# Gated-delta inverse: the diagonal blocks of 16 solved on VectorE by way of DRAM, and the attention mixer's product queued behind the matrix

## The chip, the cores and the metric

The kernel runs on one core of a Trainium2 chip. The metric is the device time of one execution in microseconds (us). The five engines of a core have queues of their own and run in order: PE (TensorE, matrix products and transposes), DVE (VectorE), ACT (ScalarE), POOL (GpSimd) and SP (SyncE, which here issues the DMAs). PSUM is the memory into which TensorE writes; it is used here as eight banks, in four pairs named acc, pc, pd and pa.

## The reference

A stack of four layers over 256 tokens of width 1024. Two layers, called "first" here, hold four mixers on a quarter of the width each (a: HGRN2, b: gated linear attention, c: latent attention, d: the gated delta rule), then an output product `w_out` and a feed-forward part. Two more layers of another kind follow, which the change does not touch. Mixer d computes, for each chunk of 64 tokens and each of 4 heads:

```
kb = kc * bt[..., None]
m = jnp.where(strict, jnp.einsum('nbhid,nbhjd->nbhij', kb, kc) * lmask, 0.0)
rhs = jnp.concatenate([vc * bt[..., None], kb * jnp.exp(b)[..., None]], axis=-1)
sol = lax.linalg.triangular_solve(m + eye, rhs, left_side=True, lower=True, unit_diagonal=True)
u, w = sol[..., :dv], sol[..., dv:]
a_qk = jnp.einsum('nbhid,nbhjd->nbhij', qc, kc) * lmask
...
v_new = u_ - jnp.einsum('bhcd,bhdv->bhcv', w_, state)
o = (jnp.einsum('bhcd,bhdv->bhcv', q_ * jnp.exp(b_)[..., None], state)
     + jnp.einsum('bhij,bhjv->bhiv', a_, v_new))
```

The kernel takes chunks of 128 tokens, so there are 2 chunks and 4 heads: 8 unit lower triangular matrices of 128x128 to be inverted in each first layer.

## The kernel before

**Weights.** All weights are fp32 and come from DRAM through SP's queue into `raw` (three buffers, 512 KB each at the most). ACT rounds each to `wh` (L302), VectorE or POOL makes the rest `wl` = raw - wh (L305), and a product is three passes on TensorE (`mm3`, L331 to L333): wh with the high part, wl with the high part, wh with the low part. A buffer of `raw` comes free when its `wl` is made, and the next weight's DMA waits for that.

**What sets the order.** A tile scheduler, driven by a simulated timeline, puts each engine's instructions in one fixed order. The mixers are generators that are advanced in phases (`PLAN1` = d, b, a, c; `RUN1`): d's preparation, b's projection, d's inverse, a's projection, b's end, c, c's attention, a's end. Each engine then does its list in order, so an instruction that waits holds back all behind it on that engine.

**Mixers a and b** are the work that surrounds d on VectorE: for each level of a tree over the chunk `gl_e` (L723, L729) and `gl_r` (L735) are made on VectorE, multiplied on TensorE (L745, L753) and written under a mask into `gl_a` (copies under a predicate, L762); then the values are applied (L770, L771), and the head's norm (L603 to L610: `hn_sq` on ACT, `hn_ssq`, `hn_y`, `hn_o` on VectorE) and the transposed result `mT` (L417 to L420) follow.

**Mixer d.** For each chunk t, L1129 multiplies K and Q with the transposed K, and L1130, L1131 multiply by the decay: `MT`, the negated strict part, transposed, and `AT` for the output. The transposed K (`kT`, L1104 and L1118) is laid out with zeros, so that a product over all 128 partitions takes one head's 64. The inverse goes by doubling of blocks: `V` begins as the identity with the blocks of 2 filled in (L1148, L1157), `T` holds the transposed diagonal blocks that a level needs (L1147, L1156, L1153). Six levels follow, w = 2, 4, ..., 64. A level below 32 multiplies MT by T (L1178), masks the result to `X` (L1179, on VectorE), multiplies V by X (L1193) and adds it into V (L1194, VectorE), then transposes V (L1199) into the next T (L1201, ACT). The levels 32 and 64 do the same on partial products and end on ACT (L1170, L1173, L1186, L1190). The output begins at L1207 and L1212 for chunk 0 and goes on with the state S0 (L1220), wT (L1229) and chunk 1.

**Mixer c** begins with a product of the input by 416 columns (`pz`), whose PSUM banks are one of `acc` and one of `pa`, in rotation.

Of the kernel before, what the change touches and what calls it, by code (L numbers as in the profile page):

```python
# [26 lines left out]
NEG = -1e30  # L27
# [34 lines left out]
def host_constants():  # L62
# [79 lines left out]
class K:  # L142
    def __init__(self, ctx, tc, a):
# [7 lines left out]
        self.ps = e(tc.tile_pool(name="ps", bufs=1, space=PSUM))  # L151
        self.units, self.made, self.nexti, self.emitted = [], {}, 0, 0
# [740 lines left out]
    def mixer_c(self, l, xT):  # L893
# [12 lines left out]
        pz = self.tm(xT, (("c", l), 2, 416))  # L906
# [93 lines left out]
    def mixer_d(self, l, xT):  # L1000
# [3 lines left out]
        code = [self.z([128, 16], "b_code", "b") for _ in range(2)]  # L1004
# [38 lines left out]
        def prep(t):  # L1043
# [5 lines left out]
            nbeta = self.s(4, "d_nbeta")  # L1049
            nc.vector.tensor_scalar(nbeta, beta, -1.0, None, op0=OP.mult)  # L1050
# [42 lines left out]
            nc.vector.tensor_tensor(kb, qk[:, 4:8], bc4(nbeta, 64), OP.mult)  # L1093
# [9 lines left out]
            kT = self.z([128, 2, 2, 128], "d_kT")  # L1103
            nc.gpsimd.memset(kT, 0.0)  # L1104
# [11 lines left out]
            for par in range(2):  # L1116
                rr = slice(par * 64, par * 64 + 64)
                nc.scalar.activation(kT[rr, par], p2[rr, :2], AF.Copy)  # L1118
            if t:
                o["qeT"] = self.z([128, 2, 128], "d_qeT")  # L1120
                nc.scalar.activation(o["qeT"], p2[:, 2:], AF.Copy)
# [22 lines left out]
        for t in range(2):  # L1144
            T[t] = self.z([128, 4, 64], "d_T")
            V[t] = self.z([128, 4, 128], "d_V")
            nc.gpsimd.tensor_copy(part(T[t], 2), half(mb(self.ident), 2, 0))  # L1147
            nc.gpsimd.tensor_copy(V[t], mb(self.ident))  # L1148
        for t in range(2):
            MT = st[t]["MT"]  # L1150
            p = four()
            for h in range(4):
                nc.tensor.transpose(p[:, h], MT[:, h], self.ident)  # L1153
            at = lambda i, n: self.cu[:, i * 64:i * 64 + 64].rearrange("p (b s) -> p b s", s=n)[:, None].to_broadcast(
                [128, 4, 64 // n, n])
            nc.vector.copy_predicated(part(T[t], 2), at(6, 2), half(p, 2, 0))  # L1156
            nc.vector.copy_predicated(half(V[t], 1, 1), at(5, 1), half(MT, 1, 1))  # L1157
        for lv in range(6):
            w = 2 << lv
            X = [None] * 2  # L1160
            for t in range(2):
# [17 lines left out]
                nc.vector.tensor_tensor(half(X[t], w, 0), part(p, w), half(mb(ms[:, lv * 128:lv * 128 + 128]), w, 0), OP.mult)  # L1179
            for t in range(2):  # L1180
                p = self.pt()[:, :256].rearrange("p (h i) -> p h i", h=4)
                if w >= 32:
# [11 lines left out]
                nc.vector.tensor_tensor(v, v, part(p, w), OP.add)  # L1194
# [37 lines left out]
        nc.scalar.activation(wT[:64], pw, AF.Copy)  # L1232
# [573 lines left out]
```

## Time and profile before

| | |
|---|---|
| median of 3 runs | 1531.69 us (1529.27 to 1532.72) |
| profiled execution, its own time | 1533.64 us |
| its span | 1531.9 us |
| busy: PE / DVE / ACT / POOL | 1477.8 / 1061.0 / 841.5 / 282.0 us |
| mean granted clock of TensorE | 0.992 |
| layer 0: first d_MT (L1130); first matmul of the output (L1207) | 86.5; 151.1 us |
| layer 0: the last masked copy of mixer a (L762) ends | 160.5 us |
| layer 1: first d_MT (L1130); L1207 | 472.4; 543.4 us |

The profiled execution took 1533.64 us, of which 1531.9 us lie between its first and its last instruction. The busy time of PE counts matmuls whose ends are modelled, so that a stretch with PE at 99% need not be at TensorE's peak. The two first layers are alike in their order; the stretches that the change touches lie at about 85 to 160 us and 470 to 553 us.

### The profile page before, as it was taken

To read this page: it belongs to the slowest core of one execution; us is meant where nothing else is said; L and a number is where in the kernel's file an instruction comes from. 1 tells how busy PE (TensorE), PEld (TensorE's weight loads), DVE (VectorE), ACT (ScalarE), POOL (GpSimd) and SP (SyncE) were. 2 spreads that over 40 slices of the span, in tenths; PEclk is the share of its full clock that TensorE was granted. 3 is DMA by queue.
4 is the path that set the end of the run, shared out by engine and by line. 5 is a ranking of instruction groups with operands and counts; after the bars stand their busy time and mean duration, and the time that the engine had idled before them with its cause. 6 is when DMAs were issued, how large, how long until landed. Compare 5 with 4: busy or idle time off the path is not lost.

```text
span 1531.9 us, 23533 instructions
## 1 busy us (share of the span) xinstructions
PE 1477.8 (96%) x8718; PEld 1278.7 (83%) x8727; DVE 1061.0 (69%) x1895; ACT 841.5 (55%) x1528; POOL 282.0 (18%) x379
## 2 busy tenths in 40 slices
PE   7999999999998999999999989999999999999998
PEld 7988888888897987888878878888877888788886
DVE  6897467767689666767676876566656695666655
ACT  5735356556565444655545674544554675544553
POOL 1553210000244332000042132000024231100010
PEclk9999999999999999999999999999999999999999
DMA  7523046666452213666646343666654543466663
GB/s 239 150 85 111 30 139 182 200 188 207 134 167 82 83 58 111 191 189 187 204 132 196 95 138 104 192 193 190 209 184 127 164 125 110 131 193 190 190 203 105
DMA packets 156417, 233.98 MB, mean 153 GB/s; under 512 B 11700, under 2 KB 118158, under 8 KB 156302
## 3 DMA queue, kind: packets, MB, share of 16 engines
q1 hardware_dynamic: 156302, 232.48, 49.2%
q8 instruction: 68, 1.11, 0.3%
q14 instruction: 47, 0.39, 0.1%
HBM read 231.40 MB, written 1.05 MB: 152 GB/s over the span
## 4 chain that ended last, share of the span: by engine, by line
PE 75%; DVE 12%; ACT 5%; POOL 2%; DMA 2%; issue 2%; SPq 0%; ACTq 0%; DVEq 0%; POOLq 0%
PE pa L377 8%; PE pd L377 8%; PE acc L333 6%; PE acc L331 6%; PE acc L332 6%; PE pc L331 5%; PE pc L333 5%; PE pc L332 5%; PE pa L378 4%; PE pd L378 4%; DVE wl L305 3%; PE pa L331 3%; PE pa L333 3%; PE pa L332 3%; DMA raw<-in_w_in_dram 2%
## 5 line engine op out<-in xcount | busy, mean ns | idle before, releaser
L305 DVE TENSOR_TENSOR wl<-raw,wh 128x1024 fp32r<-128x1024 f32 (+4 forms) x424 | 484.7, 1151 | 308.9 <-ACT wh L302 307.3
L302 ACT ACTIVATE wh<-raw 128x1024 fp32r<-128x1024 f32 (+4 forms) x420 | 432.9, 1035 | 368.0 <-PE pc L333 90.9
L305 POOL TENSOR_TENSOR wl<-raw,wh 128x1024 fp32r<-128x1024 f32 (+1 forms) x26 | 61.7, 2373 | 640.6 <-ACT wh L302 640.5
L377 PE MATMUL pa<-xT,wh 128*128 128x512 f32 x392 | 146.0, 398 | 0.0
L377 PE MATMUL pd<-xT,wh 128*128 128x512 f32 x392 | 145.7, 397 | 0.0
L378 PE MATMUL pa<-xT,wl 128*128 128x256 f32 x392 | 110.2, 281 | 0.2 <-DVE wl L305 0.2
L378 PE MATMUL pd<-xT,wl 128*128 128x256 f32 x392 | 110.2, 281 | 0.0
L377 PEld LDWEIGHTS pd<-xT,wh 128*128 128x128 f32 x392 | 73.7, 188 | 15.3
L377 PEld LDWEIGHTS pa<-xT,wh 128*128 128x128 f32 x392 | 73.7, 188 | 13.9
L332 PE MATMUL acc<-wl,f_h 128*128 128x512 f32 x200 | 78.0, 390 | 0.0
L332 PE MATMUL pc<-wl,f_h 128*128 128x512 f32 x200 | 77.8, 389 | 0.0
L333 PE MATMUL acc<-wh,f_l 128*128 128x512 f32 x200 | 77.3, 391 | 0.4 <-DVE f_l L1302 0.4
L333 PE MATMUL pc<-wh,f_l 128*128 128x512 f32 x200 | 77.5, 389 | 0.0
L378 PEld LDWEIGHTS pa<-xT,wl 128*128 128x128 f32 x392 | 74.1, 189 | 3.7 <-DVE wl L305 0.4
L378 PEld LDWEIGHTS pd<-xT,wl 128*128 128x128 f32 x392 | 74.1, 189 | 3.3
L331 PE MATMUL acc<-wh,xT 128*128 128x512 f32 (+4 forms) x200 | 70.8, 357 | 1.4 <-ACT xT L512 1.1
L332 PE MATMUL acc<-wl,xT 128*128 128x512 f32 (+4 forms) x200 | 70.6, 354 | 1.5 <-DVE wl L305 1.5
L331 PE MATMUL pc<-wh,f_h 128*128 128x512 f32 x200 | 71.4, 390 | 0.0
L333 PE MATMUL acc<-wh,xT 128*128 128x512 f32 (+4 forms) x200 | 70.2, 353 | 0.8 <-DVE xT L514 0.8
L331 PE MATMUL acc<-wh,f_h 128*128 128x512 f32 x200 | 67.0, 391 | 0.0
L331 PE MATMUL acc<-wh,mT 128*128 128x512 f32 (+2 forms) x136 | 51.1, 384 | 1.4 <-ACT mT L512 1.1
L332 PE MATMUL acc<-wl,mT 128*128 128x512 f32 (+2 forms) x136 | 51.1, 376 | 0.0
(660 smaller groups left out, 3843.4 us busy)
## 6 DMA issues: line engine op xcount, KB each, us to landing
raw<-in_w_in_dram SPq DMA_DIRECT2D x84, 512.0 KB, 3.7
raw<-in_w_mlp_up_dram SPq DMA_DIRECT2D x64, 512.0 KB, 3.8
raw<-in_w_mlp_down_dram SPq DMA_DIRECT2D x64, 512.0 KB, 3.6
raw<-in_ffn_w_gate_dram SPq DMA_DIRECT2D x44, 512.0 KB, 3.6
raw<-in_ffn_w_up_dram SPq DMA_DIRECT2D x44, 512.0 KB, 3.6
raw<-in_ffn_w_down_dram SPq DMA_DIRECT2D x44, 512.0 KB, 3.6
raw<-in_w_out_dram SPq DMA_DIRECT2D x32, 512.0 KB, 3.5
raw<-in_w_ple_gate_dram SPq DMA_DIRECT2D x16, 512.0 KB, 4.8
```

The source lines that it names most:

```text
L302: nc.scalar.activation(h[:, p], raw[:, p], AF.Copy)
L305: e.tensor_tensor(l[:, p], raw[:, p], h[:, p].bitcast(F), OP.subtract)
L331: t.matmul(out, ah, bh, start=first, stop=False, skip_group_check=True)
L332: t.matmul(out, ah, bl, start=False, stop=False, skip_group_check=True)
L333: t.matmul(out, al, bh, start=False, stop=last, skip_group_check=True)
L377: t.matmul(out[f], h[:, k, c], xT.both[:, :, kk], start=kk == 0, stop=False, skip_group_check=True)
L378: t.matmul(out[f][:, 1], l[:, k, c], xT[0][:, kk], start=False, stop=kk == 7, skip_group_check=True)
```

## The change

1. MT is no longer negated (`kb` takes beta; the signs go to VectorE's subtraction at the end of a level and to a scale of -1 in three copies on ACT).
2. `kT` is no longer laid out with zeros: one copy by ACT, and the products take slices of 64 partitions. POOL's memset of kT goes.
3. The diagonal blocks of 16 (64 of them in a layer: 8 matrices with 8 blocks) are inverted on VectorE. MT is written to a DRAM buffer `scr` (two DMAs of 256 KB), read back as `Z`, one block to a partition (1024 runs of 64 bytes), solved in `Y` by seven steps of two small instructions and four instructions of 64x512, and Y is written to a second DRAM buffer `scv` (1024 runs of 64 bytes). `V` is loaded from there (two DMAs of 256 KB). Levels w = 2, 4 and 8, and the copies that began them, go; w = 16, 32 and 64 stay as they were.
4. `scv` is set to zero once at the start, by four DMAs of 129 KB each. The tables lose 384 columns of bf16 in `cb` and 64 of fp32 in `cu`.
5. Mixer c's product takes both banks of `acc` and stands, on TensorE, behind the last product of L1129 (`lastmat`). The tile `code` gets buffers of its own.

```
+        zero = self.z([128, 258], "zero", "d")
+        nc.gpsimd.memset(zero, 0.0)
+        for i in range(4):
+            nc.sync.dma_start(self.at(self.scv, i * 128 * 258, [[258, 128], [1, 258]]), zero)
...
-        pz = self.tm(xT, (("c", l), 2, 416))
+        with self.tc.issue_after(self.lastmat.ins):
+            pz = self.tm(xT, (("c", l), 2, 416), outs=self.first_banks("acc"))
...
-                    nc.tensor.matmul(p[:, f], kT[:, par, f], qkT[:, f], start=True, stop=True)
+                    self.lastmat = nc.tensor.matmul(p[:, f], kT[rr, f], qkT[rr, f], start=True, stop=True)
...
+        dense = lambda m, t: self.at(m, t * 4 * 129 * 128, [[128, 128], [129 * 128, 4], [1, 128]])
+        blocks = lambda m: self.at(m, 0, [[16 * 129, 64], [128, 16], [1, 16]])
+        for t in range(2):
+            nc.sync.dma_start(dense(self.scr, t), st[t]["MT"])
+        Z, Y = self.z([64, 256], "d_Z"), self.z([64, 256], "d_Y")
+        nc.sync.dma_start(Z.rearrange("p (j r) -> p j r", r=16), blocks(self.scr))
+        nc.gpsimd.tensor_copy(Y, self.cb[:64, 512:768])
+        tmp, U = self.z([64, 512], "d_tmp"), self.z([64, 64], "d_U")
+        for r in range(1, 8):
+            p = tmp[:, :2 * r * r].rearrange("p (a c j) -> p a c j", a=2, c=r)
+            nc.vector.tensor_tensor(p, view(Z, r, [[136, 2], [0, r], [16, r]]), view(Y, 0, [[136, 2], [16, r], [1, r]]), OP.mult)
+            nc.vector.tensor_reduce(view(Y, r, [[136, 2], [16, r]]), p, AX.X, OP.add, negate=True)
+        p = tmp.rearrange("p (c r j) -> p c r j", c=8, r=8)
+        nc.vector.tensor_tensor(p, view(Y, 0, [[16, 8], [0, 8], [1, 8]]), view(Z, 8, [[0, 8], [1, 8], [16, 8]]), OP.mult)
+        nc.vector.tensor_reduce(U.rearrange("p (c i) -> p c i", c=8), p, AX.X, OP.add)
+        nc.vector.tensor_tensor(p, view(U, 0, [[8, 8], [0, 8], [1, 8]]), view(Y, 136, [[0, 8], [1, 8], [16, 8]]), OP.mult)
+        nc.vector.tensor_reduce(view(Y, 8, [[16, 8], [1, 8]]), p, AX.X, OP.add, negate=True)
+        nc.sync.dma_start(blocks(self.scv), Y.rearrange("p (c r) -> p c r", r=16))
...
         for t in range(2):
-            T[t] = self.z([128, 4, 64], "d_T")
             V[t] = self.z([128, 4, 128], "d_V")
-            nc.gpsimd.tensor_copy(part(T[t], 2), half(mb(self.ident), 2, 0))
-            nc.gpsimd.tensor_copy(V[t], mb(self.ident))
-        for t in range(2):
-            MT = st[t]["MT"]
+            nc.sync.dma_start(V[t], dense(self.scv, t))
             p = four()
             for h in range(4):
-                nc.tensor.transpose(p[:, h], MT[:, h], self.ident)
...
-            nc.vector.copy_predicated(part(T[t], 2), at(6, 2), half(p, 2, 0))
-            nc.vector.copy_predicated(half(V[t], 1, 1), at(5, 1), half(MT, 1, 1))
-        for lv in range(6):
+                nc.tensor.transpose(p[:, h], V[t][:, h], self.ident)
+            T[t] = self.z([128, 4, 64], "d_T")
+            nc.scalar.activation(part(T[t], 16), half(p, 16, 0), AF.Copy)
+        for lv in range(3, 6):
             w = 2 << lv
```

Lines have moved by 16 or more in the changed kernel: L305 is L321 there, L735 is L751, L762 is L778, L753 is L769, L1129 to L1131 are L1140 to L1142, L1178 and L1179 are L1203 and L1204, L1193 and L1194 are L1218 and L1219.

**VectorE, layer 0, where the inverse begins.** Before, from the copy ahead of the last of the four MT (L1130) to the first mask of a level (L1179):

```order
L1157 COPY_PREDICATED d_V<-cu,d_MT 128x256
L1130 TENSOR_TENSOR d_MT<-pd,d_L 128x2x128
L1131 TENSOR_TENSOR d_AT<-pd,d_L 128x2x128
L1156 COPY_PREDICATED d_T<-cu,pd 128x256
L1157 COPY_PREDICATED d_V<-cu,d_MT 128x256
L729 TENSOR_TENSOR gl_e<-b_b 128x32x4
L735 TENSOR_TENSOR gl_r<-gl_e,gl_q 128x256 x6
L1179 TENSOR_TENSOR d_X<-pd,cb 128x128x2
```

In the changed kernel, from the last MT on (L1160 and L1161 are the first two small steps of the solution, L1160 the first that needs Z):

```order
L1141 TENSOR_TENSOR d_MT<-pd,d_L 128x2x128
L1142 TENSOR_TENSOR d_AT<-pd,d_L 128x2x128
L751 TENSOR_TENSOR gl_r<-gl_e,gl_q 128x256 x2
L321 TENSOR_TENSOR wl<-raw,wh 128x832
L321 TENSOR_TENSOR wl<-raw,wh 128x1024
L1160 TENSOR_TENSOR d_tmp<-d_Z,d_Y 64x2
L751 TENSOR_TENSOR gl_r<-gl_e,gl_q 128x256 x6
L745 TENSOR_TENSOR gl_e<-b_b 128x32x4
L1161 TENSOR_REDUCE d_Y<-d_tmp 64x2
L321 TENSOR_TENSOR wl<-raw,wh 128x1024
L1160 TENSOR_TENSOR d_tmp<-d_Z,d_Y 64x8
L751 TENSOR_TENSOR gl_r<-gl_e,gl_q 128x256
```

In the place of the first masks and additions stand the steps of the solution, and more of the weights' `wl` (L321) stands among them: five of 128x1024 from here to the end of the solution, and a sixth right behind it.

**VectorE, layer 0, behind the solution.** In the changed kernel, from the last step of the solution (L1166) to the first mask of the level w = 16 (L1204):

```order
L1166 TENSOR_REDUCE d_Y<-d_tmp 64x8x8
L626 TENSOR_TENSOR hn_o<-hn_y,a_g 128x256
L321 TENSOR_TENSOR wl<-raw,wh 128x1024
L436 TENSOR_TENSOR mT<-pa,mT 128x2x128
L621 TENSOR_REDUCE hn_ssq<-hn_sq 128x4
L1011 TENSOR_TENSOR c_cn<-c_kr,cf 128x32
L1012 TENSOR_TENSOR rp_1645<-c_kr,cf 128x16
L1013 TENSOR_TENSOR rp_1645<-c_kr,cf 128x16
L624 TENSOR_TENSOR hn_y<-pa,rs 128x256
L1204 TENSOR_TENSOR d_X<-pd,cb 128x16x16
L626 TENSOR_TENSOR hn_o<-hn_y,a_g 128x256
```

These are the rows that stand on VectorE between the solution's last step and the first instruction that needs V and T.

**TensorE, layer 0.** Before, behind the last product of L1129:

```order
L1129 MATMUL pd<-d_qkT,d_kT 128x256 x2
L1153 MATMUL pd<-cf,d_MT 128x128 x4
L745 MATMUL pa<-gl_r,gl_e 128x256 x2
L1153 MATMUL pd<-cf,d_MT 128x128 x4
L1178 MATMUL pd<-d_T,d_MT 128x64 x4
L753 MATMUL pa<-gl_r,gl_e 64x128 x4
L753 MATMUL pa<-gl_r,gl_e 128x128 x8
L1178 MATMUL pd<-d_T,d_MT 128x64 x4
L1193 MATMUL pd<-d_V,d_X 128x64 x4
L753 MATMUL pa<-gl_r,gl_e 128x128 x8
```

In the changed kernel c's 48 passes (L347 to L349 on `acc`) come directly behind L1140, then the 28 matmuls of b's tree (L769) and b's values, of which these are the last:

```order
L787 MATMUL pa<-a_v,gl_a 128x64
L786 MATMUL pa<-a_v,gl_x 128x64
L787 MATMUL pa<-a_v,gl_a 128x64
L786 MATMUL pa<-a_v,gl_x 128x64
L787 MATMUL pa<-a_v,gl_a 128x64
L1180 MATMUL pd<-cf,d_V 128x128 x8
L1203 MATMUL pd<-d_T,d_MT 128x64 x8
L1218 MATMUL pd<-d_V,d_X 128x64 x4
L433 MATMUL pa<-cf,hn_o 128x128 x2
L722 MATMUL pa<-gl_q,a_k 128x256 x2
L1218 MATMUL pd<-d_V,d_X 128x64 x4
L947 MATMUL pc<-cf,c_cn 128x128 x3
```

The transposes of V (L1180) stand behind all of c's product and of b's tree, and a's first product (L722, on `a_k`) stands behind L1180.

On SP, the two writes of MT and the read of Z stand behind the first two weight DMAs of `w_out`, and the write of Y and the two loads of V behind the eighth and last of them, each in the one list and behind those above it.

## Rows read from the trace of the kernel before

**Rows 1.** The page: the span, busy time of each engine, the chain that ended last.

```profile
span 1531.9 us, 23533 instructions
...
PE 1477.8 (96%) x8718; PEld 1278.7 (83%) x8727; DVE 1061.0 (69%) x1895; ACT 841.5 (55%) x1528; POOL 282.0 (18%) x379
...
PE 75%; DVE 12%; ACT 5%; POOL 2%; DMA 2%; issue 2%; SPq 0%; ACTq 0%; DVEq 0%; POOLq 0%
```

**Rows 2.** Stretches: length, busy us of PE, PEld, DVE, ACT, POOL, PEclk, DMA share, GB/s.

```profile
0.00:30.00 30.00, 20.70 (x144) 19.85 (x145) 17.44 (x39) 17.17 (x32) 3.74 (x11) 1.00 0.83 249
86.00:160.50 74.50, 70.29 (x565) 62.58 (x563) 62.84 (x144) 31.68 (x84) 30.46 (x60) 1.00 0.27 90
472.00:552.60 80.60, 73.08 (x561) 64.90 (x559) 66.59 (x149) 33.78 (x86) 33.28 (x66) 0.96 0.25 84
110.00:120.00 10.00, 9.93 (x90) 9.69 (x89) 5.69 (x14) 2.30 (x6) 2.16 (x6) 1.00 0.09 23
120.00:130.00 10.00, 9.93 (x71) 9.55 (x71) 5.96 (x10) 4.06 (x6) 2.22 (x5) 1.00 0.22 78
160.00:170.00 10.00, 9.82 (x45) 8.16 (x45) 4.13 (x14) 4.85 (x17) 2.10 (x5) 0.66 0.01 2
```

**Rows 3.** VectorE in layer 0: start, us, line, operation, count; in brackets idle time and releaser.

```profile
95.51 0.72 DVE L1157 COPY_PREDICATED d_V<-cu,d_MT 128x256 f32<-128x256 uint8 x1
96.03 0.45 DVE L1130 TENSOR_TENSOR d_MT<-pd,d_L 128x256 f32<-128x256 f32 x1
...
97.91 2.77 DVE L735 TENSOR_TENSOR gl_r<-gl_e,gl_q 128x256 f32<-128x256 f32 x6
...
126.95 1.22 DVE L305 TENSOR_TENSOR wl<-raw,wh 128x1024 fp32r<-128x1024 f32 x1 [0.82 <-ACT wh L302]
...
159.22 1.28 DVE L762 COPY_PREDICATED gl_a<-cu,pa 128x256 f32<-128x256 uint8 x2
```

**Rows 4.** VectorE's waits from 86 to 160.4 us: total us, times, longest.

```profile
DVE wl L305 <- ACT wh L302: 2.9, 4, 1.2
...
DVE d_V L1194 <- PE pd L1193: 1.3, 3, 0.5
DVE d_X L1179 <- PE pd L1178: 0.9, 1, 0.9
```

**Rows 5.** TensorE by line and shape, 86 to 162 us: count, busy us, mean ns, idle before.

```profile
L1178 PE MATMUL pd<-d_T,d_MT 128*128 128x64 f32 x64 | 8.3, 272 | 0.8 <-DVE d_T L1156 0.8
L1193 PE MATMUL pd<-d_V,d_X 128*128 128x64 f32 x64 | 8.0, 272 | 0.0
L1199 PE MATMUL pd<-cf,d_V 128*128 128x128 f32 x40 | 5.8, 276 | 0.1
```

**Rows 6.** VectorE by line and shape, whole span, the same columns.

```profile
L625 DVE TENSOR_REDUCE sm_mx<-pc 128x2 f32<-128x512 f32 x12 | 8.1, 678 | 5.9 <-PE pc L975 4.9 <-PE pc L1627 0.9
...
L1179 DVE TENSOR_TENSOR d_X<-pd,cb 128x256 f32<-128x256 f32 x16 | 6.7, 420 | 2.0 <-PE pd L1178 1.8
L631 DVE TENSOR_SCALAR sm_nb<-sm_mx 128x2 f32<-128x2 f32 x40 | 6.7, 168 | 0.2
...
L1194 DVE TENSOR_TENSOR d_V<-d_V,pd 128x256 f32<-128x256 f32 x16 | 6.7, 418 | 3.1 <-PE pd L1193 3.0
...
L1157 DVE COPY_PREDICATED d_V<-cu,d_MT 128x256 f32<-128x256 uint8 x4 | 2.9, 720 | 0.0
...
L1156 DVE COPY_PREDICATED d_T<-cu,pd 128x256 f32<-128x256 uint8 x4 | 1.7, 430 | 0.0
```

**Rows 7.** DMA: the queue (packets, MB, share of 16 engines); issues (count, KB, us to landing).

```profile
q1 hardware_dynamic: 156302, 232.48, 49.2%
...
gain<-in_pre_ffn_g_dram SPq DMA_DIRECT2D x4, 256.0 KB, 3.6
...
out_dram<-x SPq DMA_DIRECT2D x4, 256.0 KB, 2.0
...
d_dt<-in_gdn_dt_bias_dram SPq DMA_DIRECT2D x2, 2.0 KB, 6.5
```

More of the change, by code (lines that the diff above doesn't have):

```diff
@@ L173, in masks, with at, view @@
         nc.gpsimd.tensor_copy(self.cu, t)
+        zero = self.z([128, 258], "zero", "d")
+        nc.gpsimd.memset(zero, 0.0)
+        for i in range(4):
+            nc.sync.dma_start(self.at(self.scv, i * 128 * 258, [[258, 128], [1, 258]]), zero)
+    @staticmethod
+    def at(t, offset, dims):
+        t = t[:]
+        return bass.AP(tensor=t.tensor, offset=t.offset + offset, ap=dims)
+    @staticmethod
+    def view(t, offset, dims):
+        return bass.AP(tensor=t.tensor, offset=t.offset + offset, ap=[list(t.ap[0])] + dims)
     def c(self, name):
@@ L1003, in mixer_d @@
         pz = self.tm(xT, (("dz", l), 2, 280))
-        code = [self.z([128, 16], "b_code", "b") for _ in range(2)]
+        code = [self.xp.tile([128, 16], F, name=f"code{t}", bufs=1) for t in range(2)]
         for t in range(2):
@@ L1092, in prep @@
             kb = self.z([128, 4, 64], "d_kb")
-            nc.vector.tensor_tensor(kb, qk[:, 4:8], bc4(nbeta, 64), OP.mult)
+            nc.vector.tensor_tensor(kb, qk[:, 4:8], bc4(beta, 64), OP.mult)
             if t == 0:
@@ L1115, in prep @@
             nc.scalar.activation(qkT, p1, AF.Copy)
[L1116 to L1121, printed above, removed]
+            kT = self.z([128, 4, 128], "d_kT")
+            nc.scalar.activation(kT[:, :4 if t else 2], p2[:, :4 if t else 2], AF.Copy)
+            o["qeT"] = kT
             yield
@@ L1178, in mixer_d @@
                     nc.tensor.matmul(p[:, h], st[t]["MT"][:, h], T[t][:, h], start=True, stop=True)
-                nc.vector.tensor_tensor(half(X[t], w, 0), part(p, w), half(mb(ms[:, lv * 128:lv * 128 + 128]), w, 0), OP.mult)
+                nc.vector.tensor_tensor(half(X[t], w, 0), part(p, w), half(mb(self.cb[:, 384:512]), w, 0), OP.mult)
             for t in range(2):
@@ L1193, in mixer_d @@
                     nc.tensor.matmul(p[:, h], X[t][:, h], v[:, h], start=True, stop=True)
-                nc.vector.tensor_tensor(v, v, part(p, w), OP.add)
+                nc.vector.tensor_tensor(v, v, part(p, w), OP.subtract)
             for t in range(2):
@@ L1231, in mixer_d @@
         nc.gpsimd.memset(wT[64:], 0.0)
-        nc.scalar.activation(wT[:64], pw, AF.Copy)
+        nc.scalar.activation(wT[:64], pw, AF.Copy, scale=-1.0)
         pu = self.pt()[:, :256].rearrange("p (h d) -> p h d", h=4)
```

25 lines of the change are left out of this document (10 added, 15 removed).

## The prediction

> **What bounds the kernel now.** The page comes first: TensorE is busy for 1477.8 of 1531.9 us and carries 75% of the chain that ended last, VectorE 12% [rows 1]. That says where the kernel as a whole is bound, not the stage that the change touches, so the second view is the stretches. The stage runs in layer 0 from 86 us, ahead of the first MT, to 160.5 us, the end of mixer a's last masked copy [rows 3], and in layer 1 from 472 to 552.6 us. In both TensorE and VectorE are nearly full together: PE is busy for 70.29 of 74.5 us and 73.08 of 80.6, VectorE for 62.84 and 66.59 [rows 2]. So VectorE idles 74.5 - 62.84 = 11.7 us and 80.6 - 66.59 = 14.0 us. Most of it lies in the middle: from 110 to 130 us PE is busy for 19.86 of 20 us and VectorE for 11.65 [rows 2]. There the reader sees TensorE hold VectorE up: VectorE waits for L1178 and L1193, and longest for ACT's `wh`, whose products come late [rows 4]. At both ends of the stage it is the other way round. Since VectorE's list hardly gets shorter (below), the question is what becomes of its 11.7 and 14.0 us of waiting: the change takes away waits for TensorE and puts in waits for DMAs. I count the stage's end by VectorE.
>
> **What the change removes.** On TensorE, three of four levels with L1178 and L1193 (48 of 64 matmuls of each in layer 0) and 24 of 40 transposes: 8.3 x 3/4 + 8.0 x 3/4 + 5.8 x 24/40 = 15.7 us of busy time in a layer [rows 5]. That is a bound of what TensorE gets free, and it counts only where VectorE waited for TensorE. On VectorE, six masks and six additions (0.42 each), two copies of 0.72 and two of 0.43: 12 x 0.42 + 1.44 + 0.86 = 7.3 us of durations [rows 6]; but rows overlap (the copy of 0.72 at 95.51 is followed at 96.03, after 0.52 [rows 3]; six `gl_r` take 2.77), so I take 6.0 us.
>
> **What it adds on VectorE.** Fourteen small instructions of 2 to 98 elements: between the 0.168 of a 128x2 operation and the 0.42 of 256 elements [rows 6], and nearer the first by their size: I take 0.18, 2.6 us (5.9 at the upper end). Four of 512 elements at the 0.678 of a reduction over 128x512, less the overlap, 0.65: 2.6 us [rows 6]. Together 5.2 us, so VectorE's own work falls by 0.8 us in a layer. The masked and transposed writes and the signs on ACT, POOL's memsets and the narrower K products (64 partitions, same columns) I cost at nothing: POOL is busy for 30.46 of 74.5 us and ACT for 31.68 [rows 2]. If ACT's cover were gone, one copy of kT more or less would be some 0.4 us.
>
> **The first round trip.** The last MT stood at 96.03 us with one copy (0.52 to the next start) ahead of it that is gone [rows 3]: it ends at about 96.0. MT's write: 256 KB to DRAM landed in 2.0 us after its issue [rows 7], with 0.4 for the issue 2.4. Z is 1024 pieces of 64 bytes. No row shows such pieces. From below it is a plain 256 KB transfer of 2.0; from above 6.5, the slowest small transfer of the page [rows 7]. In between: 49.2% of 16 x 1531.9 us over 156302 packets is 77 ns for a packet [rows 7], and 1024/16 = 64 of them in one DMA engine are 4.9 us. I take 4.9, because the count of pieces and not their bytes is what this transfer has much of. Z is there at 96.0 + 2.4 + 4.9 = 103.3. In VectorE's order between that MT and the first step that needs Z stand one AT, two `gl_r`, and a `wl` of 832 and one of 1024: 0.33 + 2 x 0.46 + 0.95 + 1.15 = 3.35 us, to 99.3 (`gl_r` by six in 2.77, `wl` by 1.22 less the overlap [rows 3]). VectorE stops there for 4.0 us, and behind the waiting step stand six `gl_r`, that is b's tree, for which TensorE waits next. In layer 1 there stand two `gl_e` and two `gl_r` more, and I take 2.3.
>
> **The solution and the second round trip.** From the first step to the last, VectorE has about 20.5 us of work (14 `gl_r`, 12 masked copies, four `wl`, the 18 new ones) and I allow 1 us of waits for weights, which have one free buffer at a time: Y is ready at about 103.3 + 21.5 = 124.8. Its write is again 1024 pieces: 0.4 + 4.9; then V, two loads of 256 KB, between 2.0 and 3.6 for one [rows 7], 3.9 for both with the issue; then eight transposes, ACT's copy, eight products and their semaphores, by the durations of [rows 5] at 8 in about 0.9 us: 0.9 + 0.4 + 0.9 + 0.4 = 2.6. The first X comes at 124.8 + 5.3 + 3.9 + 2.6 = 136.6. Behind the solution VectorE has only `hn_o`, a `wl`, `mT`, `hn_ssq`, three rows of c's rotation and `hn_y`, 3.0 us, before the instruction that waits; so it idles 11.8 - 3.0, about 9 us. Queued behind that wait are a's remaining tree and c's norms, since a's product on TensorE stands behind the transposes of V.
>
> [...]
>
> **The rest of the stage.** Levels 16 to 64 then run beside what VectorE still has to do of a and c; of before's idle time, 1.7 us (layer 0) and 2.8 us (layer 1) lay behind 136 and 523 us, and I add 0.5 for the late start. Idle after: 4.0 + 1.0 + 9.0 + 2.2 = 16.2 us in layer 0, 2.3 + 1.0 + 9.0 + 3.6 = 15.9 in layer 1. Against 11.7 and 14.0, and less 0.8 of work each: +3.7 and +1.1 us.
>
> **The start.** The four zero DMAs are 516 KB; the tables are 128 KB smaller. In the first 30 us the DMA engines are 0.83 full and move 249 GB/s, and PE is busy for 20.70 of 30 [rows 2]: weights are what it waits for. 388 KB at 249 GB/s are 1.6 us; nothing, if they slip into a gap, and 2.5 with four issues of 0.4 and more. I take 1.6, once. **Mixer c's product** in `acc`: I cost it at nothing by itself, since it fills what TensorE would idle behind L1140; without that cover 48 passes of some 0.35 us would be late next.
>
> **Sum.** 3.7 + 1.1 + 1.6 = 6.4 us on 1533.64, the profiled execution; the median shown is 1.95 lower, so on its footing 1531.69 + 6 = 1537.5 us.
>
> **The rivals.**
> *Faster.* The point that decides is the landing of the 64-byte transfers. At 2.0 each, Z comes at 100.4, VectorE stops for 1.1 (nothing in layer 1), Y is ready at 121.9, and X comes 0.4 + 2.0 + 3.9 + 2.6 = 8.9 later, 5.9 of it idle. Idle 1.1 + 1 + 5.9 + 2.2 = 10.2 and 0 + 1 + 5.9 + 3.6 = 10.5: -2.3 and -4.3 with the work; with the start -5.0, and if V's loads overlap at 2.4 together another -3: 1524 to 1527. For it: 256 KB landed in 2.0; against: the count of pieces. It decides below about 3 us for each.
> *No change.* The round trips last as I say but TensorE, 15.7 us lighter, catches up: a's tail, where VectorE meets two masked copies stretched to 1.28 [rows 3], is less crowded, and 2 to 3 us in a layer come back. 1531 to 1533. It is also what comes of it if VectorE's list, almost unchanged in length, is all that counts.
> [...]
>
> **How the numbers follow.** A difference under 0.2% (3 us) can't be told from none here. My forecast (1533 to 1542) has 0.42, faster 0.30, no change 0.16, slower still 0.12. A sixth of the forecast's range lies within 3 us, and a little of the faster rival: faster 0.31, same 0.22, slower 0.47. The range takes in the faster rival to its end and most of the slow one: 1523 to 1549.
>
> **What would show it.** Right: VectorE idle for about 4 us in front of the first step of the solution in layer 0 and about 9 us in front of the first mask of w = 16, with DMAs as releasers; both 64-byte transfers near 5 us; PE idle between 100 and 136 us; output of d (L1232) at 151 to 153 us, where L1207 stood at 151.1; the first weights' end some 1.6 us later. Wrong: 64-byte transfers near 2 us, or VectorE's idle time below 11 us in layer 0; or a gain in the part after the inverse, where I have counted none; or small vector instructions that take twice 0.18 us.

## The result and the profile after

The changed kernel takes 1545.43 us (median of 4 runs, 1545.21 to 1545.60) against 1532.20 for the kernel before in the same session (4 runs, 1529.27 to 1535.33): 1.009 times as long, with a 95% interval of 1.0072 to 1.0107. The profiled execution took 1545.45 us, with a span of 1543.7, 11.8 more than before.

The page of the changed kernel, the lines that answer to [rows 1]:

```profile
span 1543.7 us, 23007 instructions
...
PE 1465.0 (95%) x8478; PEld 1260.0 (82%) x8487; DVE 1057.5 (69%) x1895; ACT 838.4 (54%) x1514; POOL 281.6 (18%) x358
...
PE 75%; DVE 11%; ACT 5%; DMA 4%; POOL 2%; issue 2%; SPq 0%; ACTq 0%; DVEq 0%; POOLq 0%
```

TensorE is busy for 12.8 us less and VectorE for 3.5 less, and the span is longer: both wait more. DMA, 2% of the chain before, is 4% now. Stretches of the changed kernel follow, with the columns of [rows 2]. The second and third row are the stage in each first layer, from ahead of the first MT to the end of mixer a's last masked copy; the last two rows are parts of layer 0's stage behind the solution:

```profile
0.00:30.00 30.00, 18.50 (x118) 17.43 (x118) 16.09 (x36) 16.18 (x29) 4.21 (x12) 0.94 0.81 246
88.30:166.90 78.60, 65.09 (x450) 56.37 (x449) 61.12 (x146) 31.54 (x84) 29.80 (x53) 0.87 0.33 100
476.00:557.60 81.60, 66.52 (x450) 58.91 (x448) 65.02 (x155) 34.53 (x90) 36.77 (x56) 0.81 0.31 98
110.00:120.00 10.00, 6.02 (x39) 5.38 (x40) 9.86 (x29) 2.00 (x4) 1.47 (x3) 0.92 0.60 190
120.00:130.00 10.00, 4.43 (x21) 4.08 (x20) 6.84 (x11) 2.73 (x5) 2.63 (x6) 0.50 0.35 98
130.00:140.00 10.00, 9.68 (x47) 9.26 (x48) 4.63 (x17) 2.47 (x13) 4.65 (x13) 0.55 0.21 67
124.90:134.00 9.10, 7.64 (x36) 7.36 (x36) 3.09 (x9) 3.79 (x15) 3.50 (x10) 0.50 0.44 122
136.00:166.90 30.90, 30.77 (x268) 26.00 (x268) 23.38 (x58) 15.86 (x49) 13.37 (x23) 0.95 0.12 36
```

The stage is 78.6 us long in layer 0 (74.5 before) and 81.6 in layer 1 (80.6 before). VectorE idles 78.6 - 61.12 = 17.5 and 81.6 - 65.02 = 16.6 us, where it idled 11.7 and 14.0 [rows 2]. TensorE, at 9.93 of 10 us and a clock of 1.00 in 110 to 130 before, is busy for 6.02 and 4.43 now and its clock is granted at 0.92 from 110 us, 0.50 from 120 and 0.55 from 130; from 130.3 to 135.6 us, where V's transposes and the first products of the level 16 lie, it is 0.50. VectorE in layer 0 (the columns of [rows 3]):

```profile
97.12 0.41 DVE L1141 TENSOR_TENSOR d_MT<-pd,d_L 128x256 f32<-128x256 f32 x1
...
103.35 0.15 DVE L1160 TENSOR_TENSOR d_tmp<-d_Z,d_Y 64x2 f32<-64x2 f32 x1 [2.75 <-DMA d_Z<-scr]
...
119.70 1.02 DVE L1163 TENSOR_TENSOR d_tmp<-d_Y,d_Z 64x512 f32<-64x512 f32 x1
120.78 1.23 DVE L321 TENSOR_TENSOR wl<-raw,wh 128x1024 fp32r<-128x1024 f32 x1
...
124.22 0.67 DVE L1166 TENSOR_REDUCE d_Y<-d_tmp 64x64 f32<-64x512 f32 x1
...
126.45 1.23 DVE L321 TENSOR_TENSOR wl<-raw,wh 128x1024 fp32r<-128x1024 f32 x1 [1.24 <-ACT wh L318]
...
129.84 0.42 DVE L621 TENSOR_REDUCE hn_ssq<-hn_sq 128x4 f32<-128x256 f32 x1 [1.83 <-ACT hn_sq L619]
132.60 0.21 DVE L1011 TENSOR_TENSOR c_cn<-c_kr,cf 128x32 f32<-128x32 f32 x1 [2.34 <-ACT c_kr L936]
...
133.93 0.42 DVE L1204 TENSOR_TENSOR d_X<-pd,cb 128x256 f32<-128x256 f32 x1 [0.61 <-PE pd L1203]
```

The last MT comes at 97.12. The first step of the solution waits for Z's DMA, 2.75 us. The solution ends at 124.9, and the first mask of the level 16, which needs V, starts at 133.93; what VectorE has in between waits for ACT three times. The longer two of these waits go back to TensorE: `hn_sq` needs b's last values, and `c_kr` stands in ACT's list behind the copy of T, which needs V's transposes. TensorE's rows there:

```profile
125.36 0.66 PE L433 MATMUL pa<-cf,hn_o 128*128 128x128 f32 x2 [4.90 <-DVE hn_o L626]
...
130.32 1.97 PE L1180 MATMUL pd<-cf,d_V 128*128 128x128 f32 x8 [0.99 <-DMA d_V<-scv]
132.08 3.51 PE L1203 MATMUL pd<-d_T,d_MT 128*128 128x64 f32 x16
...
137.52 1.74 PE L722 MATMUL pa<-gl_q,a_k 128*128 128x256 f32 x4
```

The two transposes for b's `mT` (L433) come after 4.90 us of waiting for VectorE; V is there at 130.3, and its eight transposes take 1.97 us and the sixteen instructions of the level 16 3.51, at the clock of 0.50. Mixer a's first product (L722) comes behind them, at 137.5. The transfers themselves are short. In the list of DMA issues (count, KB, us to landing):

```profile
scr<-d_MT SPq DMA_DIRECT2D x4, 256.0 KB, 2.5
d_V<-scv SPq DMA_DIRECT2D x4, 256.0 KB, 2.6
...
scv<-zero SPq DMA_DIRECT2D x4, 129.0 KB, 4.7
...
d_Z<-scr SPq DMA_DIRECT2D x2, 64.0 KB, 2.9
...
scv<-d_Y SPq DMA_DIRECT2D x2, 64.0 KB, 2.5
```

The write of Y, 1024 pieces of 64 bytes, lands in 2.5 us and the read of Z in 2.9; 256 KB in pieces of 512 bytes take 2.5 and 2.6.

A ledger by places in the program, from the two traces: the first MT comes at 88.83 for 86.52 (+2.3 us); the stage of layer 0 adds 4.1; from its end to the last update of `x` behind `w_out` (206.2 before, 210.4 after) 2.2 come back; to the stage of layer 1 nothing changes (-0.2); that stage adds 1.0 and the part behind it 2.7 (`x` at 598.5 and 606.2). There the program that the change touches ends, at +7.7. But from there to the end, where every engine's order is row for row that of before, the changed kernel takes 937.5 us in place of 933.4: another 4.1 us. These are two single executions, and single executions scatter: experiment 1 below has the same program order, and its updates of `x` stand at 214.5 and 607.2. The 4.1 us of the last part lie in the products of the feed-forward parts that read `f_h` and `f_l`. Two groups, first of the kernel before and then of the changed one, by line and shape (mean ns behind the comma):

```profile
L332 PE MATMUL acc<-wl,f_h 128*128 128x512 f32 x200 | 78.0, 390 | 0.0
L332 PE MATMUL pc<-wl,f_h 128*128 128x512 f32 x200 | 77.8, 389 | 0.0
...
L348 PE MATMUL acc<-wl,f_h 128*128 128x512 f32 x200 | 79.1, 396 | 0.0
L348 PE MATMUL pc<-wl,f_h 128*128 128x512 f32 x200 | 79.0, 395 | 0.0
```

The mean is 396 and 395 ns in place of 390 and 389. The pace, the time from the start of one such matmul to that of the next, is 233.2 ns between 620 and 820 us, where the kernel before had 227.3. Of the same shape with other operands, the products of `wh` and `wl` with `xT` did not change: the median from one start to the next is 227 ns in both traces. Those with `pT`, which lies in the pool of `f_h`, went from 226.7 to 232.1 ns (mean).

### The profile page after: what moved, and what is told of

It is laid out like the page before. It is cut to its first block, busy times and chain, and to the rows that moved or that the text cites. A ratio compares the mean times of both kernels' runs of the same rounds, so it can differ in the third digit from the quotient of the medians.

```text
span 1543.7 us, 23007 instructions
## 1 busy us (share of the span) xinstructions
PE 1465.0 (95%) x8478; PEld 1260.0 (82%) x8487; DVE 1057.5 (69%) x1895; ACT 838.4 (54%) x1514; POOL 281.6 (18%) x358
## 4 chain that ended last, share of the span: by engine, by line
PE 75%; DVE 11%; ACT 5%; DMA 4%; POOL 2%; issue 2%; SPq 0%; ACTq 0%; DVEq 0%; POOLq 0%
PE pd L393 7%; PE pa L393 7%; PE acc L349 6%; PE acc L347 6%; PE acc L348 6%; PE pc L349 5%; PE pc L347 5%; PE pc L348 5%; PE pa L394 4%; PE pd L394 4%; DVE wl L321 3%; PE pa L347 2%; PE pa L348 2%; PE pa L349 2%; DVE x L502 1%
## 5 line engine op out<-in xcount | busy, mean ns | idle before, releaser
L321 DVE TENSOR_TENSOR wl<-raw,wh 128x1024 fp32r<-128x1024 f32 (+4 forms) x424 | 485.8, 1154 | 310.6 <-ACT wh L318 309.7
L321 POOL TENSOR_TENSOR wl<-raw,wh 128x1024 fp32r<-128x1024 f32 (+1 forms) x26 | 60.7, 2338 | 644.8 <-ACT wh L318 613.5
L349 PE MATMUL acc<-wh,f_l 128*128 128x512 f32 x200 | 78.4, 397 | 0.6 <-DVE f_l L1327 0.6
L349 PE MATMUL pc<-wh,f_l 128*128 128x512 f32 x200 | 78.2, 393 | 0.0
L347 PE MATMUL acc<-wh,xT 128*128 128x512 f32 (+4 forms) x216 | 76.3, 358 | 1.4 <-ACT xT L528 1.1
L349 PE MATMUL acc<-wh,xT 128*128 128x512 f32 (+4 forms) x216 | 76.2, 355 | 0.7 <-DVE xT L530 0.7
L348 PE MATMUL acc<-wl,xT 128*128 128x512 f32 (+4 forms) x216 | 75.6, 351 | 0.1
L347 PE MATMUL pc<-wh,f_h 128*128 128x512 f32 x200 | 72.2, 393 | 0.0
L347 PE MATMUL acc<-wh,f_h 128*128 128x512 f32 x200 | 67.7, 394 | 0.0
L349 PE MATMUL acc<-wh,mT 128*128 128x512 f32 (+2 forms) x136 | 50.2, 373 | 0.6 <-DVE mT L530 0.6
L347 PE MATMUL acc<-wh,mT 128*128 128x512 f32 (+2 forms) x136 | 49.4, 372 | 1.2 <-ACT mT L528 1.1
```

What stands on the lines that cost most here:

```text
L321: e.tensor_tensor(l[:, p], raw[:, p], h[:, p].bitcast(F), OP.subtract)
L347: t.matmul(out, ah, bh, start=first, stop=False, skip_group_check=True)
L348: t.matmul(out, ah, bl, start=False, stop=False, skip_group_check=True)
L349: t.matmul(out, al, bh, start=False, stop=last, skip_group_check=True)
```

## Experiments

My theories before the experiments were these: the stage is longer because TensorE ran out of work and lost its clock, and because a's tree starts behind V; the start is longer by the zero DMAs; and the products with `f_h` are slower because of where their tiles lie. The rivals are in each expectation.

**1. The addresses of before in the changed kernel.**

```
+        self.pad = self.cst.tile([128, 208], F, name="pad")
...
-        code = [self.xp.tile([128, 16], F, name=f"code{t}", bufs=1) for t in range(2)]
+        code = [self.cp.tile([128, 16], F, name=f"code{t}", bufs=1) for t in range(2)]
```

> The changed kernel with every tile of the two feed-forward parts back at its SBUF address of the kernel before (832 bytes of padding behind the tables, the code tiles at the end); the order of all engines is that of the changed kernel, row for row. Theory: the products that read f_h and f_l, 232.5 ns from one to the next in the changed kernel and 227.5 before, are slower because of where the tiles lie; then they return to 227.5 ns and about 1300 of them by 5 ns give back 4 to 7 us: 1539 to 1541 us. Rival: the pace hangs on something else (the chip's state in those runs, another neighbour); then 1545 us and 232.5 ns.

Measured: 1541.80 us (1540.31 to 1543.52), 1.0077 times before (1.0055 to 1.0099), 3.6 less than the changed kernel. That interval overlaps the changed kernel's, so the pace has to decide. It is back at that of before, 227.4 ns, as are the means:

```profile
L350 PE MATMUL acc<-wl,f_h 128*128 128x512 f32 x200 | 78.0, 390 | 0.0
L350 PE MATMUL pc<-wl,f_h 128*128 128x512 f32 x200 | 77.8, 389 | 0.0
```

From layer 1's last update of `x` to the end this execution takes 1539.1 - 607.2 = 931.9 us, where the changed kernel took 937.5. So the place of the tiles is the cause of the slower products. The 3.6 us are a little less than the 4 to 7 expected.

**2. More work for TensorE.** Behind each level of b's tree and behind its values:

```
+    def fill(self, mm, n):
+        p = self.bank("pc")
+        with self.tc.issue_after(mm.ins):
+            for _ in range(n):
+                self.nc.tensor.matmul(p, self.identb, self.cb[:, :512], start=True, stop=True)
```

> The changed kernel with 4 more bf16 products of 128x512 behind each level of mixer b's tree on TensorE, 16 behind b's first values and 4 behind its second, into a bank that nobody reads; nothing is left out. Theory: the granted clock of 0.50 to 0.55 from 120 to 140 us costs 3 to 5 us in a first layer, since the transposes of V, the level 16 and b's values all run on the path at half speed; then the clock stays near 1.0 there and the kernel comes to 1536 to 1540 us. Rival: VectorE's and ACT's chain sets the time there anyway; then the clock is up and the time within 2 us of 1545.

Measured: 1542.86 us (1539.76 to 1547.45), 2.6 less, with the runs further apart than this. The clock is 1.00 up to 120 us and 0.73 and 0.93 in the next two stretches. The theory and its rival are not told apart by this one: the gain lies between the two, and the scheduler, which sees the extra products too, also put some of VectorE's instructions in another order.

**3. The zero DMAs later.**

```
+            if l == 0 and g == 2:
+                with self.tc.issue_after(self.lastraw.ins):
+                    for i in range(4):
+                        nc.sync.dma_start(self.at(self.scv, i * 128 * 258, [[258, 128], [1, 258]]), self.zero)
```

> The changed kernel with the four DMAs that zero scv moved on the sync engine's list behind eight more weight DMAs. Theory: at the start they take 516 KB of the DMA engines' time while TensorE waits for weights; then the first MT comes some 2 us earlier (86.5 to 87 us) and the kernel takes 1543 to 1544 us. Rival: the start is later by the order of the small loads behind them and not by their bytes, or the later place costs the same again: 1545 us.

Measured: 1546.12 us (1544.12 to 1547.20): no gain. The first MT does come early, at 85.71 us, but the order of the other engines shifts with it, and the stage takes it back (the last update of `x` behind layer 0's `w_out` is at 212.2). Experiments 2 and 4, with the zero DMAs where the change put them, have the first MT at 86.77 and 86.94. Against these two the zero DMAs cost about 1.1 us at the start. What makes up the 2.3 us of the changed kernel's trace is not shown. Its clock in the first 30 us is 0.94, and 1.00 in those two, but in experiment 9 the clock there is 1.00 and the first MT comes at 88.81: the start differs by some 2 us from one execution to another with the zero DMAs in the same place.

**4. Mixer c's product as before.**

```
-        with self.tc.issue_after(self.lastmat.ins):
-            pz = self.tm(xT, (("c", l), 2, 416), outs=self.first_banks("acc"))
+        pz = self.tm(xT, (("c", l), 2, 416))
```

> The changed kernel with mixer c's product as before: banks by rotation and no place behind the last K product. Theory: the product ahead of the inverse leaves TensorE with too little work from 104 to 130 us, so the clock falls; with it back among the levels the clock stays up and the time falls by 2 to 5 us, to 1540 to 1543. Rival: without it the product waits behind V and the levels and everything of c comes later: 1547 or more.

Measured: 1538.25 us (1534.16 to 1540.27), 1.0047 times before (1.0032 to 1.0063): 7.2 us less than the changed kernel. The gain is there but not by a higher clock. The kernel's stretches at 110 and 120 us:

```profile
110.00:120.00 10.00, 4.22 (x21) 3.92 (x20) 6.22 (x14) 1.15 (x3) 2.49 (x6) 0.64 0.09 13
120.00:130.00 10.00, 8.46 (x35) 8.22 (x36) 2.13 (x6) 1.74 (x4) 1.21 (x2) 0.51 0.16 49
```

The clock is 0.64 and 0.51, as low as in the changed kernel (0.50 and 0.55 from 120 and 130 us). What differs is VectorE's list. In the changed kernel six `wl` lie between the last MT and the end of the solution (two ahead of the first step, the first of them for c's product, and four within the solution); with c's product undone there is none. The solution ends at 115.6 us for 124.9 and the first mask of the level 16 comes at 125.2 for 133.9. The weights come in one sequence through three buffers: c's product ahead of the inverse brings forward c's weights and with them those of `w_out`, and VectorE makes their `wl` in front of Y instead of behind it. VectorE's rows for the end of the solution and the first mask, in this experiment:

```profile
114.89 0.67 DVE L1165 TENSOR_REDUCE d_Y<-d_tmp 64x64 f32<-64x512 f32 x1
...
125.15 0.42 DVE L1203 TENSOR_TENSOR d_X<-pd,cb 128x256 f32<-128x256 f32 x1 [2.84 <-PE pd L1202]
```

The time is not gained in the stage itself. From the first MT to a's last masked copy it is 81.0 and 82.8 us long here, and 78.1 and 81.2 in the changed kernel. From there to the last update of `x` behind `w_out` it is 39.4 and 41.2 us, in place of 43.4 and 48.6: with V earlier, d's last products are earlier too (at 178.5 us for 182.3 in layer 0), and `w_out` behind them. That the weights' `wl` are what holds Y up is read from the two orders. The edit also moves the product on TensorE and to other banks, and no run puts the weights back by themselves.

**5 and 6. The kernel before, moved by 64 and by 32 bytes.** One line each:

```
+        self.pad = self.cst.tile([128, 16], F, name="pad")
```

> The kernel before with 64 bytes of padding behind its tables, and nothing else: every tile behind them lies 64 bytes higher, the order of all engines is the same row for row. Theory (the first experiment's): the pace of the products with f_h and f_l hangs on where the tiles lie, in the remainder by 128 bytes, which was 96 before and is 32 in the changed kernel and here; then 233 ns in place of 227.5 and 1536 to 1538 us. Rival: it is another property of the place (a boundary that one tile crosses in the changed kernel alone); then 227.5 ns and the time of before, 1531.

> The kernel before with 32 bytes of padding: every tile behind the tables now begins at a multiple of 256 bytes. If a smaller remainder reads faster, the products of both feed-forward parts come below 227.5 and 234 ns and the kernel below 1525 us; if only the remainder by 128 that before has by chance is a good one, they come to 233 ns and the kernel to 1536 to 1538.

Measured: 1531.84 us (0.9997 to 1.0021 times before) and 1530.45 (0.9966 to 0.9999). Neither is slower, so the remainder by 128 is not the property, and a rounder address gives next to nothing. In the fifth:

```profile
L333 PE MATMUL acc<-wl,f_h 128*128 128x512 f32 x200 | 78.0, 390 | 0.0
L333 PE MATMUL pc<-wl,f_h 128*128 128x512 f32 x200 | 77.9, 389 | 0.0
```

**7 and 8. The inverse on VectorE alone, with the addresses of before; and with the extra products.** These join the edits of 1 and 4, and of 1, 2 and 4; the seventh has the program order of the fourth, instruction for instruction.

> The changed kernel without its part on mixer c's product and with the feed-forward tiles at their addresses of before: what is left is the inverse on VectorE by way of DRAM. If the two effects add, 1538.3 less 4 to 5: 1533 to 1534.5 us, within 3 us of the kernel before. Rival: the first experiment's gain came from the run and not the addresses; then 1538.

> The same with the extra products on TensorE behind mixer b's levels. If the clock (0.64 and 0.51 from 110 to 130 us with c's product undone) is what the round trips still cost, it stays up and the kernel takes 1527 to 1531 us. Rival: VectorE has nothing to do there (2.1 of 10 us busy), the wait is for V, and the clock changes little: 1532 to 1535.

Measured: 1533.40 us (0.9999 to 1.0025 times before), as the sum of the two had it; and 1522.89 us (1520.87 to 1524.60), 0.9941 times before (0.9923 to 0.9960). The eighth beats both kernels. The stretches at 110 and 120 us, first of the seventh and then of the eighth:

```profile
110.00:120.00 10.00, 4.53 (x25) 4.42 (x25) 7.19 (x17) 0.77 (x2) 2.49 (x6) 0.67 0.11 18
120.00:130.00 10.00, 7.65 (x34) 7.26 (x34) 2.54 (x6) 1.53 (x4) 1.21 (x2) 0.50 0.18 52
...
110.00:120.00 10.00, 8.25 (x41) 4.71 (x39) 7.01 (x12) 0.38 (x1) 2.63 (x6) 0.83 0.31 78
120.00:130.00 10.00, 9.91 (x74) 9.27 (x74) 4.66 (x9) 3.88 (x7) 1.25 (x3) 1.00 0.13 40
```

The clock is 0.83 and 1.00 in place of 0.67 and 0.50 in the seventh, and TensorE is nearly full from 120 us on. TensorE's rows there, again the seventh first (L1181 and L1204 are V's transposes and the level 16, in the eighth L1191 and L1214; L214 are the extra products, L355 the first pass of c's product):

```profile
122.90 1.97 PE L1181 MATMUL pd<-cf,d_V 128*128 128x128 f32 x8 [2.35 <-DMA d_V<-scv]
124.66 3.52 PE L1204 MATMUL pd<-d_T,d_MT 128*128 128x64 f32 x16
...
114.94 4.90 PE L214 MATMUL pc<-cb 128*128 128x512 bf16 x16
...
122.49 1.04 PE L1191 MATMUL pd<-cf,d_V 128*128 128x128 f32 x8
123.57 2.00 PE L1214 MATMUL pd<-d_T,d_MT 128*128 128x64 f32 x16
...
125.55 0.43 PE L355 MATMUL pa<-wh,xT 128*128 128x416 f32 x1
```

The transposes and the level's sixteen instructions take 1.04 and 2.00 us, where the seventh has 1.97 and 3.52 (and the changed kernel 1.97 and 3.51): 2.4 us in a layer. On VectorE, in the eighth as in the seventh, no `wl` stands between the last MT and the masks of the level 16 (L1215; the solution's last step is L1177), and the first behind them is at 127.95 in the eighth. Four rows of the eighth:

```profile
102.94 0.15 DVE L1171 TENSOR_TENSOR d_tmp<-d_Z,d_Y 64x2 f32<-64x2 f32 x1 [0.46 <-DMA d_Z<-scr]
...
114.95 0.68 DVE L1177 TENSOR_REDUCE d_Y<-d_tmp 64x64 f32<-64x512 f32 x1
...
125.60 0.42 DVE L1215 TENSOR_TENSOR d_X<-pd,cb 128x256 f32<-128x256 f32 x1 [0.31 <-PE pd L1214]
...
127.95 1.02 DVE L329 TENSOR_TENSOR wl<-raw,wh 128x832 fp32r<-128x832 f32 x1 [1.28 <-ACT wh L326]
```

So with c's product behind the inverse, the extra products are worth 10.5 us in the two layers. How much of that is the clock is not shown. The scheduler gave the engines another order with the extra products in it: from the last MT to Y it takes 18.4 us (97.21 to 115.63) where the seventh takes 21.0 (95.99 to 117.03), and no run has the seventh's order at the eighth's clock.

**9 and 10. Which property of the place it is.** The ninth has only the code tiles at the end, without the padding; the tenth is the kernel before with 128 bytes between the pools:

```
+        self.pp = e(tc.tile_pool(name="pp", bufs=1))
         self.zp = e(tc.tile_pool(name="zp", bufs=1))
...
+        self.pad = self.pp.tile([128, 32], F, name="pad")
```

> The changed kernel with the two code tiles (128 bytes) in a pool behind all others and no padding: the weights lie 832 bytes lower than before, and f_h and f_l 832 lower too, where the changed kernel has them 704 lower. Theory after the fifth and sixth experiments: what counts is the distance between a product's weights and its other operand, in the remainder by 256 bytes (0 before, in the first, fifth and sixth, 128 in the changed kernel); then 227.5 ns, and 1540 to 1542 us as in the first. Rival: the absolute place (one f_h tile crosses 196608 bytes in the changed kernel, as here); then 233 ns and 1545.

> The kernel before with 128 bytes between the pool of the weights and activations and the pool that holds f_h and f_l; the order is that of before, row for row. Theory: the distance by 256 becomes 128, the products go from 227.5 to 233 ns, and the kernel takes 1536 to 1538 us. Rival as above: 227.5 ns and 1531.

Measured: 1541.10 us (1539.95 to 1544.46) and 1538.37 us (1535.85 to 1540.49), the latter 1.0042 times before (1.0028 to 1.0057). The pace is 227.3 ns in the ninth and 233.4 in the tenth, between 620 and 820 us. In the tenth:

```profile
L334 PE MATMUL acc<-wl,f_h 128*128 128x512 f32 x200 | 79.1, 395 | 0.0
L334 PE MATMUL pc<-wl,f_h 128*128 128x512 f32 x200 | 79.0, 395 | 0.0
```

Both go the theory's way: with the two operands at the same remainder by 256 bytes, in the ninth, the products run at 227.3 ns, and 128 bytes off, in the tenth, at 233.4. It is not the remainder of one operand by itself: by the allocation, `f_h` stands at remainder 32 in experiment 5 and in the changed kernel, fast in the one and slow in the other (means of 390 and 396 ns), and the weights stand at 160 in experiment 9 and in the changed kernel, again fast and slow (390 and 396). In the changed kernel it is the two code tiles, 128 bytes in a pool ahead of `f_h` and `f_l`, that do it, and the 7.6 us of the tenth are the largest price seen for it.

**11. Mixer c's product kept in place, with addresses and extra products.**

> The changed kernel whole (mixer c's product behind the K products), with the addresses of before and the extra products on TensorE. If addresses and clock add, 1542.9 less 4 to 5: 1538 us; against 1522.9 with c's product undone, the place of c's product alone then costs some 15 us once the clock is held. Rival: c's place cost only by way of the clock; then it comes near 1523 to 1527.

Measured: 1540.71 us (1539.49 to 1545.29), 17.8 us more than the eighth, whose edit differs by c's product alone. Its stretches:

```profile
120.00:130.00 10.00, 7.07 (x36) 4.96 (x34) 6.80 (x10) 2.76 (x4) 3.33 (x6) 0.80 0.35 98
510.00:520.00 10.00, 3.54 (x26) 2.82 (x26) 5.08 (x9) 2.34 (x7) 4.95 (x12) 0.93 0.44 119
520.00:530.00 10.00, 10.00 (x50) 9.50 (x49) 4.73 (x17) 2.57 (x12) 2.31 (x7) 0.56 0.17 51
```

In layer 0 the clock is 0.80 in the stretch from 120 us, where the changed kernel has 0.50; in layer 1 the extra products are done before the wait begins, TensorE is idle for 6.5 of 10 us from 510, and the clock falls to 0.56 after all. So it does not show what c's place costs at a clock that is fully held. From the first MT to the last update of `x` behind `w_out` this kernel takes 119.8 us in layer 0 and 131.3 in layer 1, where the eighth takes 116.4 and 119.0. Most of the 17.8 us thus arise in the layer in which the clock fell, and the expectation's rival, that c's place costs mainly by way of the clock, is not excluded by this run. What it shows is that with c's product in its early place the extra products bring 1.1 us against the first experiment, where they bring 10.5 without. The weights' `wl` in front of Y (which comes at 124.9 us here, and at 115.6 in the eighth) can be the reason, by the argument of experiment 4, where the clock was low with and without c's early product.

**12. V without waiting for the solution.**

```
-            nc.sync.dma_start(V[t], dense(self.scv, t))
+            nc.sync.dma_start(V[t], dense(self.scr, t))
```

> The eighth kernel (c's product undone, addresses of before, extra products) with V loaded from scr, where MT stands, and not from scv: the levels don't wait for the solution nor for Y's write, and the inverse is not computed; all work is still done. If what is left of VectorE's waiting for V (some 8 us in a layer) is on the path, 1507 to 1514 us. Rival: VectorE is full with the same work in another order, and the time falls by less than 4 us.

Measured: 1527.93 us (1525.11 to 1531.85), 5 us more than the eighth, not less. The first mask of the level 16 comes at 114.3 us for 124.9, and a's last masked copy in layer 0 starts at 170.2 for 162.6, since the order of everything else moved. The rival named this outcome, VectorE with the same work in another order and no gain of 4 us. But as the order changed with the edit, it does not show whether the second round trip is on the path that sets the eighth kernel's time.

## Why the prediction came out as it did

**Direction and range were right, by a sum that had the right stage and lacked a term.** Forecast were 6.4 us on the profiled execution, measured 11.8, inside the range of 1523 to 1549. The 1545.4 us lie above the forecast's own band (1533 to 1542). The range's upper end, 1549, and the 0.12 for a slower outcome were my estimates, and no run shows what they rest on: the slowest execution of any kernel here took 1547.45 us (experiment 2). Two slips of the sum are small: the rest of layer 1's stage should read 2.8 + 0.5 = 3.3 and not 3.6, and the median 1531.69 + 6.4 = 1538.1 and not 1537.5.

**The stages: right in size, much of it by luck.** Forecast idle of VectorE was 16.2 and 15.9 us, measured 17.5 and 16.6; forecast growth 3.7 and 1.1, measured 4.1 and 1.0. Two errors of opposite sign make up the sum. Z landed in 2.9 us and not 4.9, and Y's write in 2.5, so the packet count was the wrong scale and the bound from [rows 7] below, 2.0, was nearer; the waits at the two round trips were shorter than I had them (2.75 for 4.0 in front of the first step, and nothing for 2.3 in layer 1; behind the solution 9.1 - 3.09 = 6.0 for 9.0 in layer 0, and with ACT as releaser, not a DMA). The condition of the faster rival, under 3 us for each transfer, was thereby met, and the kernel still got slower, because the DMAs were not what VectorE lacked in the second half. The step "The rest of the stage" failed: from 136 us to the end of the stage VectorE idled 30.9 - 23.38 = 7.5 us, where I had 2.2. a's tree begins there behind V's transposes, at 137.5, and the longest of VectorE's waits are for its `gl_e` on ACT (3.1 us in three). The first product of d's output (L1232) came at 159.7 us, where 151 to 153 was forecast. Y at 124.8 was forecast and 124.9 measured, for the 512-element products took 1.02 us and not 0.65 while the wait ahead was shorter. The write in 64-byte pieces took 2.5 us for 64 KB, as long as 256 KB of MT in 512-byte pieces (2.5). That is a quarter of the bytes in the same time, but no run tells the pieces from a part of the landing that does not hang on size, and it did not decide anything.

**The step that failed: "Mixer c's product in acc: I cost it at nothing by itself".** It was counted as filling for TensorE behind the K products. The fourth experiment shows 7.2 us for it. The clock was as low without it (0.51 from 120 us, and 0.50 with it), and the orders point to VectorE's weights, though no run puts these back by themselves and experiment 11 leaves a share by way of the clock open: the `wl` that I counted as given work within the solution stand there only because of it, and Y comes 9.3 us later with them. I had summed them from the order without asking where they would have stood otherwise. TensorE had room for c's 48 passes behind the level 16's first products, where the eighth experiment has them (from 125.55 us).

**The term that was missing: the place of the tiles.** 4.1 us of the 11.8 lie behind the last instruction that the change touches, and 1.2 more in layer 0's feed-forward part (190.8 us from update to update of `x` before, 192.0 after). No step of the prediction looked at what the smaller tables and the moved code tiles do to addresses; the diff has both.

**The start:** 1.6 forecast and 2.3 in this trace. Other executions with the zero DMAs in the same place have 0.3 to 0.4 (experiments 2 and 4) and 2.3 (experiment 9), so the term is neither borne out nor refuted.

**The clock in the wait** has no term in the forecast's sum. The granted clock falls there (0.50 from 120 us, 0.55 from 130), and V's transposes and the first products of the level 16 run at 0.50. On the price the seventh and eighth experiments give 10.5 us with c's product undone, 2.4 of them in each layer for V's transposes and the level 16; the rest is not told apart from the other order. With c's product in place the extra work bought 2.6 and 1.1 us (second against the changed kernel, eleventh against the first), where the clock was below 1.00 in the wait (0.73 and 0.93 in the second; 0.80 in layer 0 and 0.56 in layer 1 of the eleventh). How much the clock alone costs in the changed kernel is therefore open.

**TensorE's busy time** fell by 12.8 us and not by the 31 of the bound. Some 5.5 us of the difference are the slower products (the tenth experiment, with the work of before, is busy for 1483.3 us in place of 1477.8); beside it, the stages in which the removed work stood ran at a clock of 1.00 and 0.96 [rows 2] and run at 0.87 and 0.81 now.

**Net.** The inverse on VectorE by itself, the seventh, is not distinguishable from before; with the extra products in b's tree as well it is the fastest kernel here (1522.9 us). Whether the kernel before would gain from the extra products was not tried.

## What to carry to other kernels

When a product is queued earlier, follow its weights: here, with three buffers in one sequence, they pulled later conversions forward with them, and on VectorE, which makes these, they stood ahead of what the path waits for (Y came at 124.9 us, and at 115.6 with c's product undone). When TensorE runs out of work in a wait, look at the clock of the products behind it (here 0.50, behind a stretch with 4.43 of 10 us busy), and when extra products are put in, check whether the other engines' order is still the same before putting the gain down to the clock. When a change adds or drops even 128 bytes of tiles, look at the pace of matmuls that it does not touch (here 227.3 and 233.2 ns): compare the mean of one long unchanged group in both traces before explaining the rest.

## What the runs showed of the hardware

The pace of the 128x128 by 512 matmuls that read `f_h` or `f_l` against the weights, two operands in different pools, was 227.3 ns (before, and experiment 9) and 227.4 (experiment 1) when both addresses had the same remainder by 256 bytes by the allocation, as they have in experiments 5 and 6 too (means of 390 and 389 ns, as before), and 233.2 and 233.4 ns when they were 128 bytes apart in it (changed kernel and experiment 10); other distances were not tried, and why it is so stays open. In the changed kernel a write of 1024 pieces of 64 bytes to DRAM landed in 2.5 us and a read of as many in 2.9.
